# Attention stage of a hybrid trunk: residual input by whole token tiles, output weights two blocks ahead, and a later split of the mixer's tile

## The chip, the cores and the metric

The kernel runs on one core of one Trainium2 chip. The metric is device time in microseconds (us): the median of several executions, lower being better. A profile is one more execution, taken by the hardware profiler. The core's engines are PE (TensorE matmuls, with PEld for its weight loads), DVE (VectorE), ACT (ScalarE), POOL (GpSimd) and SP (SyncE, which here only issues DMAs). Each works through a queue of its own in order and waits at the head of it; POOL issues DMAs too, from between its arithmetic. The clock of PE is granted by a throttle: 1.00 is full speed.

## What is computed

A trunk of two layers over 1024 tokens of width 1024, with 256 context tokens. Layer 0 projects its normalised input, gives eight heads to a two-dimensional neighbourhood attention, which also reads all context keys in the same softmax, and four heads to a bidirectional gated DeltaNet (the "mixer" below). Both halves are gated and go through one output projection:

```python
def even_layer(x, ctx, ...):
    hx, gate_x = adaln_in(x, c_lat, norm_g, mod_w, mod_b)
    px = hx @ w_in
    ...
    na_x = neighbourhood_attention(qx, kx, vx, kc, vc, rpb)
    dn_x, dn_c = bidir_gated_deltanet(px[..., OFF_DN:OFF_AB], ...)
    x_new = x + gate_x * ((jnp.concatenate([na_x, dn_x], axis=-1)
                           * jax.nn.silu(px[..., OFF_Z:])) @ w_out)
```

Per query of the attention:

```python
    s_win = jnp.einsum('bqhd,brqkhd->bhqrk', qr, kw) + bias
    s_ctx = jnp.einsum('bqhd,bkhd->bhqk', qr, kc)
    p = jax.nn.softmax(concatenate([s_win, s_ctx]))
    out = p_win @ v_window + p_ctx @ v_context
```

Layer 1 is a Hyena layer, and a last norm follows. The change lies in the attention of layer 0 and in that half of its output projection, `dn_x @ w_out`, that runs beside it.

## The kernel before

Most products are made of three matmuls of a number's high and low part (hi x hi, hi x lo, lo x hi), so that weights and inputs are split first: `split` casts the high part on ACT and subtracts it from the whole on POOL (or on DVE, where asked) to give the low part.

**The attention stage** is `natten`. It has 64 turns, i = 0 to 63, for 4 pairs of heads, 8 blocks of columns and the 2 heads of a pair; i = 16, 32 and 48 begin pairs 1, 2 and 3. In turn i PE computes the scores of i (`s`, from `nq`, `nkh`, `nkl`), transposes the probabilities of i-2 (`pt`, copied to `pts`), and in odd turns multiplies by the values (`pv`) for i-4 and its predecessor. DVE adds the bias and finds the maximum (line 1050), ACT takes the exponential (line 1051), ACT and DVE finish the result (`nr`, `ny`, lines 1084 to 1086). PE, PEld and DMA issues of a pair are kept in the order of the program; the compiler's scheduler may move other instructions.

**Inputs of a pair.** Per pair two heads' `nq`, `nkh`, `nkl` come in twelve half loads on POOL's DMA queue (line 1012), 0.26 to 0.33 MB each; `nbias` (two of 0.59 MB, line 1007), `bnv` (0.66 MB) and `ny` (0.52 MB) come on SP's. In the program they are issued from the fifth turn of the pair before, two a turn; each goes out once its buffer is free, and `bnv` and `ny` with the first turn of their own pair.

**The filler.** From i = 10 each turn also runs four matmuls of `dn_out`: the mixer's half of the output projection, 8 token tiles x 2 halves of 512 columns x 12 matmuls, all into one PSUM bank `do`. A half tile therefore takes three turns. Tile t's mixer input `dyr` is loaded and split into `dyh` and `dyl` one tile ahead. For a half, `dx` receives x, DVE adds the product (line 1113), and a store writes it back to `xa_d` (line 1114). `dx` is one buffer of 128 x 512, and `dyr` is taken from the ring `wor` of three buffers, which it shares with the raw weights.

**The weights.** `load_wout` brings 16 blocks `ewo_raw` of 128 x 512 (0.26 MB), counted here from 0: a load on SP, a multiply by the gate on POOL (line 1353), and a split. Blocks 0 to 3 come before turn 0, blocks 4 to 7 in turns 0 to 3, and blocks 8 to 15 in odd turns from i = 25 as the program is written; a block's load and its arithmetic are one step. Low parts are made by POOL for blocks 0, 3, 6, ..., by DVE for the others.

The result of the last pair is split into `yeh` and `yel`, which live in the pool `wl` from the stage's start on, empty until then.

Of the kernel before, what the change touches and what calls it, by code (L numbers as in the profile page):

```python
# [10 lines left out]
F32 = mybir.dt.float32  # L11
F32R = mybir.dt.float32r
# [3 lines left out]
ALU = mybir.AluOpType  # L16
# [4 lines left out]
P = 128  # L21
D = 1024
L = 1024
# [5 lines left out]
HEADS = 4  # L29
NTL = 8  # L30
# [31 lines left out]
class Kernel:  # L62
# [192 lines left out]
    def run(self):  # L255
# [45 lines left out]
        with ExitStack() as so, ExitStack() as sh:  # L301
            with ExitStack() as st:
                gate = self.pool(st, "wg").tile([P, D], F32, name="gate0")
                nc.sync.dma_start(gate, self.gate_d[0:1, :].to_broadcast([P, D]))
                wp = self.pool(st, "wo")
                ylp = self.pool(st, "wl")
                yl = [ylp.tile([P, L], F32R, name="ye" + n) for n in ("h", "l")]
                with ExitStack() as s1:
                    w = self.natten(s1, wp, yl, gate)
# [622 lines left out]

    def natten(self, st, wp, yl, gate):
# [21 lines left out]
        half = KT // 2  # L957
        wout = self.load_wout(w, wp, ap["e_w_out"], "ewo", gate,
                              [(k, h) for h in range(2) for k in range(half, KT)] +
                              [(k, h) for h in range(2) for k in range(half)], (None, nc.vector, nc.vector)[:NA_LO])  # L960
        for _ in range(half):
            next(wout)
        self.filler, self.deferred = self.dn_out(w, yp), []
        next(self.filler)
        self.pinned = True
        for i in range(n + 4):
# [18 lines left out]
            if 0 <= i - 4 < n and i % 2:  # L985
                p, j, u = tiles[i - 4]
                self.na_values(p, j, state.pop(i - 5), state.pop(i - 4), *pairs[p])
                if j == 7:
                    _, y = pairs.pop(p)
                    if p < 3:  # L990
                        nc.sync.dma_start(self.y_d[p], y)
                    else:
                        self.split(y, *yl, lo_eng=nc.vector)
        self.drain()
        self.pinned = False
        return w

    def na_unit(self, p, u, nb):

# [85 lines left out]
        nc.vector.tensor_tensor(r3, r3, yj, ALU.mult)  # L1085
        nc.vector.tensor_tensor(yj, po[:, 0, :].rearrange("p (r c) -> p r c", c=8), r3, ALU.mult)

    def dn_out(self, w, yp):

        nc, ap = self.nc, self.ap  # L1090

        def load(i):
            raw = self.wor.tile([P, HEADS, P], F32, name=f"dyr{i}", tag="wor")
            nc.sync.dma_start(raw, self.y_d[HEADS:, :, i * P:(i + 1) * P].rearrange("k p t -> p k t"))
            ys = [yp.tile([P, HEADS, P], F32R, name=f"dy{n}{i}", tag="dy" + n) for n in "hl"]
            self.split(raw, *ys)
            return ys

        nxt = load(0)
        yield  # L1100
        for i in range(NTL):
            ys, nxt = nxt, load(i + 1) if i + 1 < NTL else None
            for n in range(2):
                sl = slice(n * 512, (n + 1) * 512)
                xt = yp.tile([P, 512], F32, name=f"dx{i}_{n}", tag="dx", bufs=1)
                nc.sync.dma_start(xt, ap["x"][i * P:(i + 1) * P, sl])
# [6 lines left out]
                nc.vector.tensor_tensor(xt, xt, ps, ALU.add)  # L1113
                nc.sync.dma_start(self.xa_d[i * P:(i + 1) * P, sl], xt)

# [224 lines left out]
        nc.sync.dma_start(self.g_d[o, cb][:, 16, :], G[:, 0, 8, :])  # L1340


    def load_wout(self, w, pool, ap, name, gate, order, lo_eng=(None,)):

        nc = self.nc
        for n in range(2):
            w.append([pool.tile([P, KT, 512], F32R, name=f"{name}_{p}{n}") for p in ("hi", "lo")])
        for i, (k, n) in enumerate(order):
            sl = slice(n * 512, n * 512 + 512)
            raw = self.wor.tile([P, 512], F32, name=f"{name}_raw{k}_{n}", tag="wor")  # L1350
            nc.sync.dma_start(raw, ap[k * P:(k + 1) * P, sl])
            if gate is not None:
                nc.gpsimd.tensor_tensor(raw, raw, gate[:, sl], ALU.mult)
            self.split(raw, w[n][0][:, k, :], w[n][1][:, k, :], lo_eng=lo_eng[i % len(lo_eng)])
            yield
# [574 lines left out]
```

## Time and profile before

| | us |
|---|---|
| median of 3 runs | 1939.85 |
| lowest and highest of them | 1932.81, 1949.21 |
| the profiled execution | 1935.17 |
| its span in the trace | 1933.1 |
| the attention stage in that span, about | 985 to 1203 |

The mean granted clock of the profiled execution was 0.952. A row of a timeline gives start, length, engine, line, operation, output and inputs, and in square brackets how long the engine stood idle before it and what ended that. `SPq` is SP's queue of DMA issues: such a row is the issue, and the data lands later. Rows of the waits read: who waited, for whom, us in all, times, the longest.

### The profile page before, as it was taken

What the parts mean: (1) busy time and instruction counts of PE and PEld (TensorE: products, weight loads), DVE (VectorE), ACT (ScalarE), POOL (GpSimd) and SP (SyncE); (2) the same over time, 40 slices, a digit from 0 to 9 for tenths busy, and PEclk for the clock granted to TensorE, in tenths of its full rate; (3) what the DMA queues carried; (4) which work ended last, traced back from release to release, by engine and by line L of the source; (5) the groups of instructions that cost most, each with busy time, mean ns of one, the idle gap of its engine ahead of it and who ended that gap; (6) DMA issues with size and microseconds to landing.
All of it is one profiled execution on the core that took longest, in us unless ns stands there. A gap on an engine that the chain in (4) does not pass through costs nothing. (4 is left out here: it accounts for less than half of the span.)

```text
span 1933.1 us, 30413 instructions
## 1 busy us (share of the span) xinstructions
PE 1752.2 (91%) x11156; PEld 1424.3 (74%) x11156; DVE 1373.9 (71%) x2786; ACT 853.3 (44%) x1851; POOL 623.5 (32%) x878
## 2 busy tenths in 40 slices
PE   6798988899988998999987799888999999999998
PEld 2466755688866776788866587767888888888776
DVE  5899998557648643655564466647998998898666
ACT  4566574354535342343353344553344344434421
POOL 0765454422495767701143300330000000000310
PEclk9898988899998999999998899989999999999999
DMA  8545544313433466533499853542433442443434
GB/s 285 172 125 140 164 170 158 120 44 107 141 111 112 152 189 217 179 129 118 170 227 238 190 158 95 170 139 67 121 92 100 100 123 67 119 124 105 123 105 140
DMA packets 133232, 271.05 MB, mean 140 GB/s; under 512 B 44074, under 2 KB 66106, under 8 KB 131035
## 3 DMA queue, kind: packets, MB, share of 16 engines
q1 hardware_dynamic: 123482, 233.45, 37.2%
q0 software_dynamic: 9600, 35.66, 10.0%
q8 instruction: 88, 1.44, 0.3%
q14 instruction: 62, 0.50, 0.1%
HBM read 193.03 MB, written 76.03 MB: 139 GB/s over the span
## 5 line engine op out<-in xcount | busy, mean ns | idle before, releaser
L116 PE MATMUL hx<-h1h,w1x_hi 128*128 128x512 f32 x256 | 101.2, 395 | 0.0
L112 PE MATMUL dn<-hh,wdn_lo 128*128 128x512 f32 (+1 forms) x256 | 95.8, 376 | 5.9 <-POOL wdn_lo L105 5.9
L116 PE MATMUL hx<-h1l,w1x_hi 128*128 128x512 f32 x256 | 100.9, 394 | 0.0
L653 DVE SCALAR_TENSOR_TENSOR dacc<-dpad,convw,dacc 128x1024 f32<-128x1024 f32 (+1 forms) x80 | 83.9, 1079 | 23.9 <-ACT dacc L651 19.5
L116 PE MATMUL hx<-h1h,w1x_lo 128*128 128x512 f32 x256 | 100.7, 393 | 0.0
L756 POOL TENSOR_TENSOR sub<-Lb,Xb 80x31 f32<-80x31 f32 (+15 forms) x124 | 84.2, 679 | 36.5 <-DMA Lb<-lsc_d 18.8
L110 PE MATMUL dn<-hh,wdn_hi 128*128 128x512 f32 (+1 forms) x256 | 95.6, 373 | 0.0
L111 PE MATMUL dn<-hl,wdn_hi 128*128 128x512 f32 (+1 forms) x256 | 95.6, 373 | 0.0
L1051 ACT ACTIVATE pr<-pr,st 128x640 f32<-128x640 f32 (+1 forms) x64 | 51.3, 802 | 73.2 <-DVE st L1050 72.5
L758 POOL TENSOR_TENSOR Xb<-Xb,sub 80x31 f32<-80x31 f32 (+15 forms) x124 | 78.3, 631 | 8.4
L112 PEld LDWEIGHTS dn<-hh,wdn_lo 128*128 128x128 f32 x256 | 49.4, 193 | 14.9 <-POOL wdn_lo L105 6.1
L116 PE MATMUL hu<-h1h,w1u_lo 128*128 128x512 f32 x128 | 51.6, 403 | 4.2 <-DMA w1u_lo<-in_w 4.2
L111 PEld LDWEIGHTS dn<-hl,wdn_hi 128*128 128x128 f32 x256 | 49.3, 193 | 8.0 <-issue 0.5
L110 PEld LDWEIGHTS dn<-hh,wdn_hi 128*128 128x128 f32 x256 | 49.4, 193 | 7.9
L1160 ACT COPY fx<-fx_ps 128x512 f32<-128x512 f32 (+1 forms) x96 | 43.6, 483 | 25.7 <-PE fx_ps L121 22.3
L116 PEld LDWEIGHTS hx<-h1h,w1x_lo 128*128 128x128 f32 x256 | 48.1, 188 | 9.2 <-DMA w1x_lo<-in_w 0.2
L116 PEld LDWEIGHTS hx<-h1l,w1x_hi 128*128 128x128 f32 x256 | 48.2, 188 | 8.9
L116 PEld LDWEIGHTS hx<-h1h,w1x_hi 128*128 128x128 f32 x256 | 48.1, 188 | 8.8
L121 PE MATMUL fx_ps<-ident,ff 128*128 128x128 f32 x288 | 49.5, 298 | 5.6 <-ACT fx L1160 3.6
L1269 PE MATMUL fh<-fhh,w3s 128*128 128x512 f32 x64 | 38.9, 611 | 17.2 <-DVE fh L1271 17.2
L156 POOL DMA_DIRECT2D w1x_lo<-in_w x16 | 13.8, 865 | 124.7 <-ACT w1x_lo L154 124.7
L1293 POOL TENSOR_TENSOR fp<-fh,fh 128x1024 f32<-128x1024 f32 x16 | 39.4, 2464 | 42.3 <-ACT fh L1279 42.3
(571 smaller groups left out, 5980.0 us busy)
## 6 DMA issues: line engine op xcount, KB each, us to landing
hG<-g_d SPq DMA_DIRECT2D x16, 1088.0 KB
g_d<-G SPq DMA_DIRECT2D x16, 1024.0 KB
em_w<-in_em_w SPq DMA_DIRECT2D x24, 512.0 KB
om_w<-in_om_w SPq DMA_DIRECT2D x24, 512.0 KB
wz_raw<-in_w0z SPq DMA_DIRECT2D x16, 512.0 KB
w1x_raw<-in_w SPq DMA_DIRECT2D x16, 512.0 KB
w1x_lo<-in_w POOLq DMA_DIRECT2D x16, 512.0 KB, 7.7
wdn_raw<-in_w0dn SPq DMA_DIRECT2D x12, 512.0 KB
```

The costliest lines, as they stand in the source:

```text
L110: nc.tensor.matmul(ps, wh, xh, start=start, stop=False)
L111: nc.tensor.matmul(ps, wh, xl, start=False, stop=False)
L112: nc.tensor.matmul(ps, wl, xh, start=False, stop=stop)
L116: ins = self.nc.tensor.matmul(*args, **kw)
L121: ins = self.nc.tensor.transpose(out, x, self.ident)
L653: nc.vector.scalar_tensor_tensor(acc[:, t0:t0 + n], pad[:, o + j:o + j + n], cw[:, blk, j:j + 1], acc[:, t0:t0 + n], ALU.mult, ALU.add)
L756: nc.gpsimd.tensor_tensor(tv, Lb[:, j + 1:, j:j + 1].broadcast_to([80, m, c]), Xb[:, j:j + 1, 0:c].broadcast_to([80, m, c]), ALU.mult)
L758: nc.gpsimd.tensor_tensor(Xb[:, j + 1:, 0:c], Xb[:, j + 1:, 0:c], tv, ALU.subtract)
L1051: nc.scalar.activation(pr[:, :n], pr[:, :n], AF.Exp, bias=st[:, 0:1], scale=-1.0, accum_out=st[:, 1:2])
L1160: nc.scalar.copy(out[:, j0:j0 + m, :].rearrange("p a b -> p (a b)"), ps[:, :m * P])
L1269: nc.tensor.matmul(ps, ws[:, od, :], hh[:, sl], start=True, stop=False)
L1293: nc.gpsimd.tensor_tensor(pp[:, :L], hf[:, :L], hb[:, :L], ALU.add)
```

## The change

Four edits, all in the attention stage:

1. `dn_out` loads x by whole token tiles (128 x 1024, 0.52 MB) instead of halves, one tile ahead with the mixer's tile, into two buffers in turn. They are the two of pool `wl`; `yeh` and `yel` take the same two buffers at the end, after the filler has drained. Adds and stores stay by halves.
2. `dyr` has a buffer of its own instead of one of the ring `wor`.
3. The split of the next mixer tile is issued after the first half of the present one, while its load is issued at the tile's start as before.
4. `load_wout` gets `ahead=2`: the load of block k is issued with step k-2. Layer 1's call keeps 0.

```diff
-    def dn_out(self, w, yp):
+    def dn_out(self, w, yp, ylp):
         def load(i):
-            raw = self.wor.tile([P, HEADS, P], F32, name=f"dyr{i}", tag="wor")
+            raw = yp.tile([P, HEADS, P], F32, name=f"dyr{i}", tag="dyr", bufs=1)
             nc.sync.dma_start(raw, self.y_d[HEADS:, ...])
-            ys = [yp.tile([P, HEADS, P], F32R, name=f"dy{n}{i}", tag="dy" + n) for n in "hl"]
+            xt = ylp.tile([P, D], F32, name=f"dx{i}", tag="y" + "eo"[i % 2])
+            nc.sync.dma_start(xt, ap["x"][i * P:(i + 1) * P, :])
+            return raw, xt
+        def split(raw):
+            ys = [yp.tile([P, HEADS, P], F32R, name=f"dy{n}", tag="dy" + n) for n in "hl"]
             self.split(raw, *ys)
             return ys
...
         for i in range(NTL):
-            ys, nxt = nxt, load(i + 1) if i + 1 < NTL else None
+            if i + 1 < NTL:
+                raw, xn = load(i + 1)
             for n in range(2):
-                xt = yp.tile([P, 512], F32, name=f"dx{i}_{n}", tag="dx", bufs=1)
-                nc.sync.dma_start(xt, ap["x"][i * P:(i + 1) * P, sl])
...
-                nc.vector.tensor_tensor(xt, xt, ps, ALU.add)
-                nc.sync.dma_start(self.xa_d[i * P:(i + 1) * P, sl], xt)
+                nc.vector.tensor_tensor(xt[:, sl], xt[:, sl], ps, ALU.add)
+                nc.sync.dma_start(self.xa_d[i * P:(i + 1) * P, sl], xt[:, sl])
+                if n == 0 and i + 1 < NTL:
+                    nxt = split(raw)
+            if i + 1 < NTL:
+                ys, xt = nxt, xn
...
     def load_wout(self, w, pool, ap, name, gate, order, lo_eng=(None,), ahead=0):
+        for kn in order[:ahead]:
+            load(*kn)
         for i, (k, n) in enumerate(order):
+            for kn in order[i + ahead:i + ahead + 1]:
+                load(*kn)
+            raw = raws.pop(0)
...
                     if p < 3:
                         nc.sync.dma_start(self.y_d[p], y)
                     else:
+                        self.drain()
+                        yl = [ylp.tile([P, L], F32R, name="ye" + n, tag="y" + t) for n, t in (("h", "e"), ("l", "o"))]
                         self.split(y, *yl, lo_eng=nc.vector)
```

PE's order is the same before and after. The other queues change in this stage alone. Rows name output and input tiles with a running number, and the shape.

SP, from the middle of pair 0 to the start of pair 1 (`nbias`, `bnv`, `ny` are pair 1's; `dyr_10293` and, after, `dyr_10295` are tile 2's mixer input). Before:

```order
L1007 DMA nbias_9896<-in_na_bias 128x1152
L1007 DMA nbias_9922<-in_na_bias 128x1152
L1094 DMA dyr_10081<-y_d 128x4x128
L1094 DMA dyr_10293<-y_d 128x4x128
L1114 DMA xa_d<-dx_0_10087 128x512
L1106 DMA dx_1_10180<-in_x 128x512
L1020 DMA bnv_10277<-nv_d 128x1280
L1022 DMA ny_10279<-zz_d 128x1024
L1094 DMA dyr_10500<-y_d 128x4x128
```

After:

```order
L1363 DMA ewo_raw_0_9853<-in_e_w_out 128x512
L1363 DMA ewo_raw_0_9875<-in_e_w_out 128x512
L1007 DMA nbias_9900<-in_na_bias 128x1152
L1007 DMA nbias_9926<-in_na_bias 128x1152
L1120 DMA xa_d<-dx_9803 128x512
L1020 DMA bnv_10279<-nv_d 128x1280
L1022 DMA ny_10281<-zz_d 128x1024
L1363 DMA ewo_raw_0_10599<-in_e_w_out 128x512
L1363 DMA ewo_raw_0_10677<-in_e_w_out 128x512
L1120 DMA xa_d<-dx_9803 128x512
L1094 DMA dyr_10500<-y_d 128x4x128
L1097 DMA dx_10297<-in_x 128x1024
```

Weight blocks 8 and 9 (9853, 9875) now stand ahead of pair 1's `nbias`; before, nothing of theirs was there. `bnv` and `ny` follow the first store at once instead of the second half's x load. The load of x tile 2 (10297) stands ahead of block 12 (10753) and behind both stores of tile 0 (`dx_9803`), whose buffer it takes.

POOL, behind the twelve loads of pair 1 (`nq_10422` and the rows like it are pair 2's). Before:

```order
L105 TENSOR_TENSOR ewo_lo_9778<-ewo_raw_1_9849,ewo_hi_9777 128x512
L105 TENSOR_TENSOR dyl_10084<-dyr_10081,dyh_10083 128x512
L105 TENSOR_TENSOR dyl_10296<-dyr_10293,dyh_10295 128x512
L1012 DMA nq_10422<-nq_d 64x1024
L1012 DMA nkh_10423<-nk_d 64x1280
L1012 DMA nkl_10424<-nk_d 64x1280
L1012 DMA nq_10422<-nq_d 64x1024
L1012 DMA nkh_10423<-nk_d 64x1280
L1353 TENSOR_TENSOR ewo_raw_0_10603<-ewo_raw_0_10603,gate_9715 128x512
```

After (the row of three dots leaves out six more of pair 2's loads):

```order
L105 TENSOR_TENSOR ewo_lo_9776<-ewo_raw_1_9823,ewo_hi_9775 128x512
L1375 TENSOR_TENSOR ewo_raw_0_9853<-ewo_raw_0_9853,gate_9715 128x512
L1375 TENSOR_TENSOR ewo_raw_0_9875<-ewo_raw_0_9875,gate_9715 128x512
L105 TENSOR_TENSOR dyl<-dyr_10295,dyh 128x512
L1012 DMA nq_10422<-nq_d 64x1024
L1012 DMA nkh_10423<-nk_d 64x1280
...
L1012 DMA nkl_10454<-nk_d 64x1280
L1012 DMA nq_10452<-nq_d 64x1024
L105 TENSOR_TENSOR ewo_lo_9774<-ewo_raw_0_9875,ewo_hi_9773 128x512
L1375 TENSOR_TENSOR ewo_raw_0_10599<-ewo_raw_0_10599,gate_9715 128x512
L1375 TENSOR_TENSOR ewo_raw_0_10677<-ewo_raw_0_10677,gate_9715 128x512
```

The multiplies of blocks 8 and 9 (9853, 9875) stand right behind pair 1's loads, and block 10's (10599) behind ten of pair 2's, where block 8's stood behind five.

ACT, around the exponentials of i = 14 (`pr_10219` before, `pr_10221` after) and i = 15 (`pr_10243`, `pr_10245`). Before:

```order
L1051 ACTIVATE pr_10219,st_10218<-pr_10219,st_10218 128x512
L1064 COPY pts_10227<-pt_3_10233 128x256
L102 CAST dyh_10295<-dyr_10293 128x512
L1051 ACTIVATE pr_10243,st_10242<-pr_10243,st_10242 128x512
L1064 COPY pts_10251<-pt_3_10257 128x256
```

After:

```order
L1051 ACTIVATE pr_10221,st_10220<-pr_10221,st_10220 128x512
L1064 COPY pts_10229<-pt_3_10235 128x256
L102 CAST ewo_hi_9773<-ewo_raw_0_9853 128x512
L102 CAST dyh<-dyr_10295 128x512
L1051 ACTIVATE pr_10245,st_10244<-pr_10245,st_10244 128x512
L102 CAST ewo_hi_9773<-ewo_raw_0_9875 128x512
```

The cast of block 8's high part stands between the two exponentials, ahead of the mixer's cast, which was alone there.

More of the change, by code (lines that the diff above doesn't have):

```diff
@@ L306, in run @@
                 ylp = self.pool(st, "wl")
-                yl = [ylp.tile([P, L], F32R, name="ye" + n) for n in ("h", "l")]
                 with ExitStack() as s1:
-                    w = self.natten(s1, wp, yl, gate)
+                    w, yl = self.natten(s1, wp, ylp, gate)
                 hp = self.pool(sh, "h1p", side="right")
@@ L930, in dn_finish, with natten @@
         self.defer(FILL_LOAD[min(hd + 1, 3)] - 1, out)
-    def natten(self, st, wp, yl, gate):
+    def natten(self, st, wp, ylp, gate):
         nc, ap = self.nc, self.ap
@@ L959, in natten @@
                               [(k, h) for h in range(2) for k in range(half, KT)] +
-                              [(k, h) for h in range(2) for k in range(half)], (None, nc.vector, nc.vector)[:NA_LO])
+                              [(k, h) for h in range(2) for k in range(half)], (None, nc.vector, nc.vector)[:NA_LO], ahead=2)
         for _ in range(half):
             next(wout)
-        self.filler, self.deferred = self.dn_out(w, yp), []
+        self.filler, self.deferred = self.dn_out(w, yp, ylp), []
         next(self.filler)
@@ L992, in natten @@
                     else:
+                        self.drain()
+                        yl = [ylp.tile([P, L], F32R, name="ye" + n, tag="y" + t) for n, t in (("h", "e"), ("l", "o"))]
                         self.split(y, *yl, lo_eng=nc.vector)
-        self.drain()
         self.pinned = False
-        return w
+        return w, yl
     def na_unit(self, p, u, nb):
@@ L1340, in filter_spectrum, with load_wout @@
         nc.sync.dma_start(self.g_d[o, cb][:, 16, :], G[:, 0, 8, :])
-    def load_wout(self, w, pool, ap, name, gate, order, lo_eng=(None,)):
+    def load_wout(self, w, pool, ap, name, gate, order, lo_eng=(None,), ahead=0):
         nc = self.nc
@@ L1347, in load_wout, with load @@
             w.append([pool.tile([P, KT, 512], F32R, name=f"{name}_{p}{n}") for p in ("hi", "lo")])
+        raws = []
+        def load(k, n):
+            raw = self.wor.tile([P, 512], F32, name=f"{name}_raw{k}_{n}", tag="wor")
+            nc.sync.dma_start(raw, ap[k * P:(k + 1) * P, n * 512:n * 512 + 512])
+            raws.append(raw)
+        for kn in order[:ahead]:
+            load(*kn)
         for i, (k, n) in enumerate(order):
             sl = slice(n * 512, n * 512 + 512)
-            raw = self.wor.tile([P, 512], F32, name=f"{name}_raw{k}_{n}", tag="wor")
-            nc.sync.dma_start(raw, ap[k * P:(k + 1) * P, sl])
+            for kn in order[i + ahead:i + ahead + 1]:
+                load(*kn)
+            raw = raws.pop(0)
             if gate is not None:
```

3 lines of the change are left out of this document (2 added, 1 removed).

## Prediction

> **What bounds the kernel now.** I read the page first, then the windows over the attention stage, the waits in it, and the timelines of PE, SP and POOL.
>
> ```profile
> PE 1752.2 (91%) x11156; PEld 1424.3 (74%) x11156; DVE 1373.9 (71%) x2786; ACT 853.3 (44%) x1851; POOL 623.5 (32%) x878
> ...
> PEclk9898988899998999999998899989999999999999
> DMA  8545544313433466533499853542433442443434
> ```
>
> PE is busy for 91% of the span, so a gain must come from places where PE is not. The DMA row has one nearly full place, slices 21 to 23 (9, 9, 8), about 1015 to 1110 us: the attention stage. In windows (columns: stretch and length, busy time and count of PE, PEld, DVE, ACT, POOL, then granted clock, DMA share, GB/s) it reads:
>
> ```profile
> 985.00:1009.00 24.00, 20.84 (x159) 16.84 (x160) 18.83 (x48) 14.34 (x34) 13.95 (x11) 0.86 0.65 222
> 1009.00:1029.00 20.00, 18.20 (x147) 15.17 (x145) 10.31 (x31) 10.00 (x26) 10.25 (x17) 0.91 1.18 225
> 1029.00:1075.00 46.00, 29.20 (x213) 24.35 (x210) 21.31 (x57) 14.02 (x35) 16.33 (x20) 0.82 0.98 240
> 1075.00:1097.00 22.00, 21.80 (x182) 18.29 (x181) 13.16 (x36) 10.81 (x28) 10.51 (x13) 0.90 0.48 123
> 1097.00:1153.00 56.00, 47.68 (x393) 40.50 (x394) 30.34 (x86) 21.38 (x56) 5.87 (x7) 0.94 0.69 186
> 1153.00:1190.00 37.00, 37.00 (x329) 31.28 (x328) 26.38 (x76) 17.84 (x47) 2.02 (x2) 1.00 0.27 90
> ```
>
> From 1029 to 1075 PE works 29.2 of 46 us while the DMA engines are full at 240 GB/s; by 1153 it is full at clock 1.00. The waits of the stage (us in all, times, longest):
>
> ```profile
> DVE dx L1113 <- DMA dx<-in_x: 28.8, 5, 12.2
> PE do L116 <- DVE dx L1113: 25.3, 5, 10.3
> POOL ewo_raw L1353 <- DMA ewo_raw<-in_e_w_out: 37.9, 10, 15.0
> ACT ewo_hi L102 <- POOL ewo_raw L1353: 10.9, 7, 2.7
> ACT dyh L102 <- PE do L116: 3.7, 5, 0.9
> ```
>
> PE's in-order queue stands 25.3 us behind the residual add, and the add behind a load of x. The five places, after the last matmul ahead of the first:
>
> ```profile
> 1029.61 0.28 PE L116 MATMUL s<-nkl,nq 128*128 128x256 f32 x1
> ...
> 1040.21 0.80 PE L116 MATMUL do<-ewo_hi,dyh 128*128 128x512 f32 x1 [10.32 <-DVE dx L1113]
> ...
> 1073.46 0.80 PE L116 MATMUL do<-ewo_hi,dyh 128*128 128x512 f32 x1 [6.48 <-DVE dx L1113]
> ...
> 1093.75 0.50 PE L116 MATMUL do<-ewo_hi,dyh 128*128 128x512 f32 x1 [0.20 <-DVE dx L1113]
> ...
> 1109.82 0.80 PE L116 MATMUL do<-ewo_hi,dyh 128*128 128x512 f32 x1 [6.74 <-DVE dx L1113]
> ...
> 1137.84 0.51 PE L116 MATMUL do<-ewo_hi,dyh 128*128 128x512 f32 x1 [1.58 <-DVE dx L1113]
> ```
>
> The first is the head of i=16, where pair 1 starts. The cause of it, from SP's and DVE's timelines:
>
> ```profile
> 1020.37 0.33 SPq L1114 DMA_DIRECT2D xa_d<-dx  x1
> ...
> 1031.22 0.35 SPq L1106 DMA_DIRECT2D dx<-in_x  x1
> ...
> 1039.46 0.69 DVE L1113 TENSOR_TENSOR dx<-dx,do 128x512 f32<-128x512 f32 x1 [12.22 <-DMA dx<-in_x]
> ```
>
> There is one `dx` buffer. Its store goes out at 1020.37, the next load only when that has landed, 10.9 us later, and the load takes 8.2 us more; two trips through full DMA engines stand between two half tiles. After each long wait the clock is halved:
>
> ```profile
> 1040.20:1045.10 4.90, 4.89 (x16) 4.12 (x17) 2.95 (x10) 1.09 (x3) 1.17 (x1) 0.50 0.86 300
> 1073.50:1079.20 5.70, 5.70 (x33) 4.64 (x33) 1.80 (x6) 1.29 (x3) 1.27 (x1) 0.50 0.54 155
> 1109.80:1113.40 3.60, 3.58 (x12) 3.11 (x13) 2.38 (x8) 0.92 (x2) 0.00 (x0) 0.50 0.29 111
> ```
>
> **The parts, and their sum.** (a) x by whole tiles, one tile ahead, in two buffers: the load no longer waits for the store just made, but for the one of the tile before. All five waits go: -25.3 us. (b) The 14.2 us at clock 0.50 would be 7.8 at the 0.91 of the window from 1009: -6.4 us. Ends of (a) and (b): 0, if the DMA engines are the true bound, and -31.7.
>
> (c) A new stall at i=17. The first keys of pair 1 come through POOL's queue, the bias and values through SP's:
>
> ```profile
> 1004.03 0.90 SPq L1007 DMA_DIRECT2D nbias<-in_na_bias  x2
> ...
> 1031.62 0.43 SPq L1020 DMA_DIRECT2D bnv<-nv_d  x1
> ...
> 1009.23 0.55 POOL L1012 DMA_DIRECT2D nq<-nq_d  x1
> ...
> 1020.05 0.51 POOL L1012 DMA_DIRECT2D nkl<-nk_d  x1 [1.79 <-DMA nq<-nq_d]
> 1020.58 1.30 POOL L105 TENSOR_TENSOR ewo_lo<-ewo_raw,ewo_hi 128x512 fp32r<-128x512 f32 x1
> ...
> 1028.93 0.54 POOL L1012 DMA_DIRECT2D nq<-nq_d  x1
> ...
> DMA to landing us min/median/max: 11.8/11.8/11.8
> ```
>
> The last row is of the load issued at 1020.05: pair 1's twelve loads end at 1031.85, behind a stall that hid them. In the changed order nbias (1.18 MB) stands on SP behind weight blocks 8 and 9 (0.26 MB each) that were not there, so it moves from 1004 into the time of the twelve loads; bnv and ny come right behind the first store instead of at 1031.6. From 1010.5 the twelve (3.67 MB), nbias, the two blocks, a mixer tile (0.26) and a store (0.26) are 5.9 MB, at 0.24 MB/us 24.6 us: the last key lands at about 1035.5 by this estimate. PE, no longer held at 1029.9, wants it at the head of i=17, about 1031.5. So 4 us, and about 2 for the clock behind it. Ends: 0 (the old 1031.85) and 10 (the whole first stall back, by a path of its own). I take +6, between, since the bytes are counted.
>
> (d) The weights. Blocks 10 to 15 are multiplied by the gate on POOL, cast on ACT in the stretch i=18 to 27, where in the changed order a cast stands ahead of the softmax exponential of the same turn. Their loads share SP's queue with x loads that wait for stores, so SP itself blocks: the load of tile 2 waits for both stores of tile 0, the second landing at about 1042 (1031 + 10.9), and blocks 12 to 15 and pair 2's nbias stand behind it. Before, POOL waited 37.9 us for raw blocks and ACT 10.9 for POOL, all beside other work. Ends: 0 and the 10.9; I take +6, since SP's queue still has these waits and PE is now ahead of them by the 16.8 us of the first two stalls.
>
> (e) At nothing: eight x loads fewer on SP (8 x 0.33 us of issue, SP not on the path); the mixer's split put after the first half, whose ACT cast waited for PE for 3.7 us in five places already, and whose result is needed 12 matmuls later; the two whole x tiles at the start (0.8 MB more before 1009, where the DMA share is 0.65; ends -2 and +2); and the last pair's split, which now waits for the last stores since it takes the x buffers:
>
> ```profile
> 1179.11 0.32 SPq L1114 DMA_DIRECT2D xa_d<-dx  x1
> ...
> 1202.63 1.22 DVE L105 TENSOR_TENSOR yel<-ny,yeh 128x1024 fp32r<-128x1024 f32 x1 [1.11 <-ACT yeh L102]
> ```
>
> Even 10.9 us after it that store has landed at 1190, 12 us ahead of need. The tail keeps its pace, two turns of i in 5.55 us: these rows are four pairs of turns apart, 22.21 us, with PE full, so nothing else can shorten it.
>
> ```profile
> 1152.72 0.29 DVE L1085 TENSOR_TENSOR nr<-nr,ny 128x128 f32<-128x128 f32 x1 [1.36 <-ACT nr L1084]
> ...
> 1174.93 0.29 DVE L1085 TENSOR_TENSOR nr<-nr,ny 128x128 f32<-128x128 f32 x1 [1.19 <-ACT nr L1084]
> ```
>
> Sum: -25.3 - 6.4 + 6 + 6 = -19.7. Against the profiled execution's 1935.17 us (span 1933.1, 2.1 around it) that is 1915.5. That execution is 4.7 under the median of three, 1939.85, inside their spread of 16 us; I add half of it, 2.3: 1918.
>
> A check by bytes: 20 us at 225, 46 at 240 and 22 at 123 GB/s are 18.2 MB from 1009 to 1097. At 240 throughout they take 76 us, so at most 12 of those 88 us can go; the two later stalls with their half clock (6.7 + 1.6 + 1.6) add 10. So -22 is about the floor, which agrees with -19.7 and not with -31.7.
>
> How the two queues share, in 1029:1075 (packets, MB, share of the 16 engines):
>
> ```profile
> q1 hardware_dynamic: 4192, 7.10, 54.5%
> q0 software_dynamic: 1018, 3.87, 43.3%
> ```
>
> POOL's queue q0 gets 43% beside SP's q1. [...]
>
> **Rivals.** *B, the DMA engines bound it.* The stalls of 1029 to 1097 come back as waits for keys, bias or values; only what the later stalls cost goes, about 10. For it: shares of 1.18 and 0.98. Against: 0.48 in 1075:1097, so there is slack just behind. Time: 1935.2 + 2.3 - 10 = 1928.
>
> *C, all is hidden.* The keys land at 1031.85 as before, and the weights' waits stay beside other work: -31.7, 1906. For it: the twelve loads start first in their queue. Against: the bytes.
>
> *D, slower: ACT's order.* ACT's cast of weight block 8 now stands ahead of the exponential of i=15, its multiply on POOL behind all twelve loads of pair 1; block 10's cast stands ahead of that of i=20, its multiply behind ten of pair 2's. POOL has had only eight loads under way at a time, so a slow landing holds the multiply, the cast, the exponential, and then PE. The exponential of i=15 ran here:
>
> ```profile
> 1027.54 0.72 ACT L1051 ACTIVATE pr<-pr,st 128x512 f32<-128x512 f32 x1
> ```
>
> At the pace seen (eleven steps from 1009.23 to 1020.05) the tail of another block (1.3), the multiply (1.3) and the cast (0.6) end at 1023.8, in time. If SP's traffic halves that pace, the twelfth issue comes at 1031 and the cast ends at 1034: 7 us late, and again for pair 2, with 5 of half clock behind both, on top of (c) and (d) and with the first two stalls of (a) not gained (16.8, and 4.8 of clock): -31.7 + 21.6 + 12 + 19 = +21, 1958. It decides when the twelfth issue is later than about 1024. For it: a share over 1. Against: nbias is the only large transfer that moves into that time.
>
> That the change does not do what it says I leave out: the order shows the loads moved.
>
> **Chances.** Mine 0.53, B 0.20, C 0.20, D 0.07. The likeliest one's own range, from (c) and (d) at 9 to 20 in place of 12 and 3 us either way for the runs, is 1909 to 1928. To hold eight in ten it reaches into C and B: 1904 to 1935. A measurement of this kernel tells about 1% from no change: 1920.5 is that bound. Faster: two thirds of mine and 0.9 of C, 0.53; slower: the half of D beyond 1959, 0.04; the rest, with B, 0.43.
>
> **What would show it.** (a): no wait of `do` on the add over 1 us; the add has x long before. (b): no stretch at 0.50 near 1040, 1073 and 1110. (c): a wait of PE's scores at i=17 on the load of nkh or nkl, 3 to 8 us, followed by a low clock. (d): waits of ACT's ewo_hi on POOL of over 2 us each between i=18 and 27, and exponentials late behind them. B shows as scores waiting over 8 us on nkl, nbias or bnv with the DMA share at 1; C as PE full from 1029; D as an exponential at i=15 or 20 behind an ewo_hi cast, with POOL's multiply behind its loads. The forecast is wrong if the windows outside 985 to 1203 move by more than 3 us, which nothing here accounts for.

## The result, and the profile after

The changed kernel took 1914.18 us (median of 4 runs, 1912.35 to 1919.9) against 1940.62 us of the kernel before (4 runs): a ratio of 0.987, 95% interval 0.982 to 0.992. The forecast was 1918. The profiled execution of the changed kernel took 1915.67 us. One execution among the experiments below, of the kernel with two further edits, took 2816.59 us at a mean clock of 0.608 and is left out of its row. The changed kernel's page, from the first two parts:

```profile
PE 1743.7 (91%) x11156; PEld 1422.0 (74%) x11156; DVE 1379.5 (72%) x2786; ACT 853.8 (45%) x1851; POOL 624.6 (33%) x878
...
PEclk9799978899999998999998999999999999999999
DMA  8445544313434367534389854533442443444424
```

PE has the same 11156 matmuls and is busy 8.5 us less (1752.2 before), which fits less time at half clock (the middle's mean clock, below, is 0.95 where it was 0.84). The DMA row is nearly as full there as it was (8, 9, 8 for 9, 9, 8).

The same stretches as before, in windows:

```profile
985.00:1009.00 24.00, 18.09 (x143) 14.08 (x144) 18.13 (x49) 16.36 (x39) 18.40 (x18) 0.93 0.68 227
1009.00:1029.00 20.00, 18.34 (x158) 15.51 (x156) 13.37 (x38) 10.04 (x26) 10.33 (x15) 1.00 1.19 237
1029.00:1075.00 46.00, 36.00 (x284) 29.59 (x285) 25.94 (x64) 17.88 (x44) 18.18 (x19) 0.93 1.00 246
1075.00:1097.00 22.00, 22.00 (x193) 18.89 (x192) 14.68 (x43) 9.57 (x25) 7.49 (x13) 1.00 0.94 217
1097.00:1153.00 56.00, 55.98 (x482) 47.84 (x482) 37.70 (x107) 25.75 (x68) 2.56 (x2) 1.00 0.56 170
```

From 1075 on PE is full at clock 1.00; of the stretches before, 1029 to 1075 has the most time without a matmul, 10 us. Fixed times mix the two kernels' progress, so from here the stage is cut by its own turns: from the exponential of i=0 to that of i=10 (the start), on to that of i=28 (the middle), and on to the last split, `yel` (the tail). Windows with these bounds, first of the kernel before:

```profile
987.63:1013.22 25.59, 22.37 (x162) 17.80 (x162) 19.54 (x52) 16.46 (x40) 18.17 (x19) 0.87 0.68 209
1013.22:1087.48 74.26, 56.24 (x429) 47.44 (x430) 35.52 (x97) 27.52 (x70) 26.21 (x31) 0.84 0.93 213
1087.48:1202.63 115.15, 103.19 (x900) 86.55 (x898) 68.20 (x196) 50.42 (x129) 15.46 (x20) 0.97 0.52 143
```

And of the changed kernel:

```profile
985.21:1009.92 24.71, 19.01 (x148) 14.78 (x149) 18.84 (x49) 16.36 (x39) 19.32 (x20) 0.93 0.70 224
1009.92:1075.41 65.49, 53.83 (x440) 44.73 (x439) 38.80 (x102) 27.92 (x70) 27.59 (x32) 0.95 1.06 244
1075.41:1180.32 104.91, 101.52 (x905) 85.89 (x903) 68.41 (x196) 50.07 (x128) 12.97 (x18) 1.00 0.56 153
```

The stage went from 215.0 to 195.1 us: 0.9 less in the start, 8.8 in the middle, 10.2 in the tail. The span outside it is 1718.1 and 1718.6 us. So the whole difference of these two executions lies in the stage. In the middle the DMA engines run at 244 GB/s with a share of 1.06: 16.0 MB in 65.5 us, where it was 15.8 MB in 74.3.

The waits of the stage now (us in all, times, longest):

```profile
PE s L116 <- DMA nkh<-nk_d: 6.1, 1, 6.1
...
PE do L116 <- DVE dx L1119: 2.6, 2, 1.7
PE s L116 <- DMA nkl<-nk_d: 2.1, 1, 2.1
...
ACT ewo_hi L102 <- POOL ewo_raw L1375: 5.0, 4, 2.0
ACT dyh L102 <- DMA dyr<-y_d: 5.7, 3, 2.8
```

PE's 25.3 us behind the add are 2.6, and the add itself waits for x nowhere: the row of 28.8 us that the kernel before had is gone from the list. A wait of 8.1 us for keys is new. It stands in PE's timeline where the prediction put it, at i=17:

```profile
1033.40 0.55 PE L116 MATMUL s<-nkh,nq 128*128 128x256 f32 x1 [6.06 <-DMA nkh<-nk_d]
1036.03 0.55 PE L116 MATMUL s<-nkl,nq 128*128 128x256 f32 x1 [2.08 <-DMA nkl<-nk_d]
...
1064.48 0.50 PE L116 MATMUL do<-ewo_hi,dyh 128*128 128x512 f32 x1 [1.74 <-DVE dx L1119]
```

The 1.74 us of the last row are no wait for x, although the row names the add. From the timelines of POOL, ACT and DVE:

```profile
1059.61 1.29 POOL L1375 TENSOR_TENSOR ewo_raw<-ewo_raw,gate 128x512 f32<-128x512 f32 x1 [1.56 <-DMA ewo_raw<-in_e_w_out]
...
1060.93 0.62 ACT L102 CAST ewo_hi<-ewo_raw 128x512 fp32r<-128x512 f32 x1 [1.04 <-POOL ewo_raw L1375]
...
1061.58 1.11 DVE L105 TENSOR_TENSOR ewo_lo<-ewo_raw,ewo_hi 128x512 fp32r<-128x512 f32 x1 [1.76 <-ACT ewo_hi L102]
...
1063.76 0.67 DVE L1119 TENSOR_TENSOR dx<-dx,do 128x512 f32<-128x512 f32 x1
```

The load of weight block 13 came late, and the add stood in DVE's queue behind that block's low part; it started without idle time before it. PE's idle time in the middle is 65.5 - 53.8 = 11.7 us: the 8.1 us for keys, these 1.7, 0.9 behind another add that stood in DVE's queue, and 0.9 behind ACT.

Two windows behind the wait for keys show the clock: at half, then partly so, and full from 1040.8 on.

```profile
1033.40:1036.00 2.60, 0.55 (x1) 0.26 (x1) 0.00 (x0) 0.00 (x0) 0.51 (x1) 0.50 1.18 253
1036.00:1040.80 4.80, 4.77 (x36) 3.97 (x36) 1.46 (x4) 0.81 (x2) 1.02 (x2) 0.69 1.26 232
```

The first and last of pair 1's twelve loads in POOL's timeline, and the landing of the last one:

```profile
1006.03 0.55 POOL L1012 DMA_DIRECT2D nq<-nq_d  x1
...
1015.98 0.51 POOL L1012 DMA_DIRECT2D nkl<-nk_d  x1 [1.95 <-DMA nq<-nq_d]
...
DMA to landing us min/median/max: 19.9/19.9/19.9
```

They are issued 3.2 us earlier than before and end at 1035.9, 29.9 us after the first issue instead of 22.6. The two queues between 1009 and 1035, by the view of the DMA queues (packets, MB, share), of the changed kernel:

```profile
q0 software_dynamic: 878, 3.37, 60.2%
q1 hardware_dynamic: 828, 2.78, 58.1%
```

In the kernel before the same stretch read:

```profile
q0 software_dynamic: 1230, 4.71, 98.0%
q1 hardware_dynamic: 1260, 1.01, 19.6%
```

POOL's queue moved 4.71 MB in 26 us before and 3.37 after, because SP's queue, which the old stall had kept nearly empty, now runs beside it; the run with pair 0's bias below tests this. Their shares went from 98.0 and 19.6% to 60.2 and 58.1%.

And SP's timeline has the longest time from a store to the load that needs its buffer:

```profile
1024.55 0.33 SPq L1120 DMA_DIRECT2D xa_d<-dx  x1
1025.10 0.38 SPq L1094 DMA_DIRECT2D dyr<-y_d  x1
1049.26 0.33 SPq L1097 DMA_DIRECT2D dx<-in_x  x1
```

The load of x tile 2, which needs tile 0's last store landed, goes out 24.7 us after that store. What SP's queue moved from 1007.8 to 1049.3:

```profile
q1 hardware_dynamic: 1471, 3.76, 52.8%
```

From 1007.9 to 1025.5 it had been given 3.7 MB (`nbias` 1.18, `bnv` 0.66, `ny` 0.52, two weight blocks, two stores and a mixer tile of 0.26 each). So the store seems to have waited its turn behind these; this is worked out from the two sums, and no run separates it. No add waited for this load, but the last four weight blocks stand behind it in SP's queue.

### The profile page after: what moved, and what is told of

The parts are those of the page before. It is cut to its first block, busy times and chain, and to the rows that moved or that the text cites. A ratio compares the mean times of both kernels' runs of the same rounds, so it can differ in the third digit from the quotient of the medians.

```text
span 1913.7 us, 30399 instructions
## 1 busy us (share of the span) xinstructions
PE 1743.7 (91%) x11156; PEld 1422.0 (74%) x11156; DVE 1379.5 (72%) x2786; ACT 853.8 (45%) x1851; POOL 624.6 (33%) x878
## 5 line engine op out<-in xcount | busy, mean ns | idle before, releaser
L652 DVE SCALAR_TENSOR_TENSOR dacc<-dpad,convw,dacc 128x1024 f32<-128x1024 f32 (+1 forms) x80 | 83.8, 1078 | 23.6 <-ACT dacc L650 19.3
L757 POOL TENSOR_TENSOR Xb<-Xb,sub 80x31 f32<-80x31 f32 (+15 forms) x124 | 86.3, 696 | 8.4
L755 POOL TENSOR_TENSOR sub<-Lb,Xb 80x31 f32<-80x31 f32 (+15 forms) x124 | 76.0, 613 | 35.0 <-DMA Lb<-lsc_d 21.0
L1171 ACT COPY fx<-fx_ps 128x512 f32<-128x512 f32 (+1 forms) x96 | 43.5, 483 | 28.4 <-PE fx_ps L121 24.9
L116 PE MATMUL hu<-h1h,w1u_hi 128*128 128x512 f32 x128 | 51.5, 402 | 0.8 <-ACT hpu L1632 0.8
```

The source lines that it names most:

```text
L116: ins = self.nc.tensor.matmul(*args, **kw)
L652: nc.vector.scalar_tensor_tensor(acc[:, t0:t0 + n], pad[:, o + j:o + j + n], cw[:, blk, j:j + 1], acc[:, t0:t0 + n], ALU.mult, ALU.add)
L755: nc.gpsimd.tensor_tensor(tv, Lb[:, j + 1:, j:j + 1].broadcast_to([80, m, c]), Xb[:, j:j + 1, 0:c].broadcast_to([80, m, c]), ALU.mult)
L757: nc.gpsimd.tensor_tensor(Xb[:, j + 1:, 0:c], Xb[:, j + 1:, 0:c], tv, ALU.subtract)
L1171: nc.scalar.copy(out[:, j0:j0 + m, :].rearrange("p a b -> p (a b)"), ps[:, :m * P])
```

## The experiments

The theory to begin with: two x buffers give the gain; pair 1's keys, slowed by SP's traffic, take part of it back. Rivals: the other edits carry the gain; the DMA engines bound the middle whatever the order. "Ratio" is to the kernel before on the same chip, with its 95% interval (its median on the chips of the experiments was 1936.55, 1936.75 and 1938.17 us); start, middle and tail are those of one profiled execution each, in us, and no kernel was profiled twice.

| kernel | median | ratio (interval) | start + middle + tail |
|---|---|---|---|
| before | 1940.62 | 1 | 25.6 + 74.3 + 115.1 |
| changed | 1914.18 | 0.987 (0.982 to 0.992) | 24.7 + 65.5 + 104.9 |
| x edit alone | 1923.77 | 0.992 (0.989 to 0.995) | 21.9 + 73.8 + 106.3 |
| weights ahead alone | 1941.29 | 1.002 (1.000 to 1.004) | 22.3 + 81.1 + 117.3 |
| changed, weights not ahead | 1910.99 | 0.988 (0.985 to 0.992) | 23.5 + 69.7 + 104.6 |
| changed, split at load | 1918.34 | 0.991 (0.988 to 0.994) | 23.7 + 71.7 + 104.8 |
| changed, x by halves | 1926.3 | 0.994 (0.992 to 0.997) | 27.1 + 71.2 + 106.5 |
| changed, values late | 1922.41 | 0.993 (0.990 to 0.995) | 24.2 + 68.5 + 112.8 |
| changed, inputs from turn 0 | 1916.36 | 0.990 (0.987 to 0.993) | 22.7 + 69.2 + 105.2 |
| changed, cast on POOL | 1917.47 | 0.989 (0.986 to 0.992) | 24.3 + 65.6 + 104.6 |
| changed, both of these | 1920.65 | 0.992 (0.989 to 0.995) | 24.1 + 77.2 + 104.6 |
| changed, pair 0's bias | one run, 1910.16 | | 23.6 + 66.4 + 104.6 |
| changed, pair 0's keys | one run, 1904.77 | | 25.8 + 52.7 + 104.6 |
| changed, six stores left out | one run, 1931.44 | | 25.0 + 72.4 + 104.6 |

The span outside the stage differs between these executions from 1712.4 to 1727.3 us, which is why the stage's parts tell more than single totals. How far the middle differs between executions of one kernel is not known.

**The x edit alone** (`dn_out` as changed, but `dyr` from the ring, split with its load, weights not ahead).

> Only the first edit on the kernel before: x by whole tiles into two buffers; the mixer's tile is in the ring and split with its load, no weights ahead. Theory (this edit carries the whole gain): stage 194 to 201 us (before 215.0, after 195.1), 1911 to 1920. Rival (the other three edits together carry a part): stage 205 or more, 1925 or more.

Stage 202.0, 1923.77 us: between the two theories. The tail has nearly the whole gain (106.3 against 115.1), the middle none. The waits in the middle say why, of ACT for POOL's weight blocks and of POOL for their loads:

```profile
ACT ewo_hi L102 <- POOL ewo_raw L1373: 19.0, 9, 7.1
```

```profile
POOL ewo_raw L1373 <- DMA ewo_raw<-in_e_w_out: 50.2, 10, 15.1
```

ACT waited 5.0 us in the changed kernel. The weights come later here, exponentials stand behind their casts, and PE waited 8.4 us for ACT's copies behind those. Three edits are left out at once; that it is the mixer's tile in the ring of three is likely, but not shown.

**Weights ahead alone** (`load_wout` as changed, on the kernel before).

```diff
-                              ..., (None, nc.vector, nc.vector)[:NA_LO])
+                              ..., (None, nc.vector, nc.vector)[:NA_LO], ahead=2)
```

> The kernel before with only the weight blocks loaded two ahead. Theory (the gain comes from the two x buffers): no gain, waits of do on the add 20 to 30 us as before, stage 212 to 220 us, 1935 to 1945. Rival (the weights' lead carries part): stage under 208, 1930 or less.

No gain, as the theory had it; the stage was 220.8 us, just over its range. PE's waits on x fell from 25.3 to 16.2 us, and this one took their place, as ACT waited for `dyr`:

```profile
PE do L116 <- ACT dyh L102: 12.3, 1, 12.3
```

In the order of this kernel ten weight blocks go out before the mixer's tile 1, where eight did, and that tile's load stands in SP's queue behind the second half's x load, which went out at 1032.97, 18.5 us after the store that it waited for. Whether a buffer of its own for `dyr` would have brought it forward was not tested alone.

**Weights not ahead**, the other three edits kept.

```diff
-                              ..., (None, nc.vector, nc.vector)[:NA_LO], ahead=2)
+                              ..., (None, nc.vector, nc.vector)[:NA_LO])
```

> The changed kernel with the weight blocks not loaded ahead (the other three edits stay). Theory (two x buffers give the gain, about 32 us of waits and half clock; the keys of pair 1 take some of it back): about as the change, 1912 to 1919 us, stage from the first exponential to the last split 195 +- 3 us (before 215.0, after 195.1), wait of the scores at i=17 still 5 to 9 us, perhaps 1 to 2 us shorter because blocks 8 and 9 (0.52 MB) stand behind the bias. Rival (the lead of the weights is part of the gain): POOL waits for raw blocks again as before (37.9 us in the stage) and the exponentials come late for it, stage 200 us or more, 1919 or more.

As the theory had it in the stage (197.8), and in time a little under its range (1910.99). The scheduler brings blocks 8 and 9 forward by itself, to 1003.9 (1003.1 in the changed kernel). The wait for keys was 3.1 + 1.7 us, but a wait of `do` for a weight block, 3.2 us, preceded it. The ratios of this kernel and the changed one overlap: the lead is worth nothing that the times show, though the middle of this one execution is 4.2 us longer.

**The split back at its load.**

```diff
-                raw, xn = load(i + 1)
+                nxt, xn = load(i + 1)
...
-                if n == 0 and i + 1 < NTL:
-                    nxt = split(raw)
```

> The changed kernel with the mixer's split put back to its load. Theory: worth nothing either way, stage 195 +- 2 us, 1912 to 1918; the only trace of it is the ACT cast dyh that waits 2.8 us for its tile ahead of the exponential of i=21, which may come a turn earlier and wait 1 to 3 us longer. Rival (the later split keeps ACT free): casts waiting for dyr in front of exponentials in several places, stage 200 or more.

Stage 200.2 against 195.1, 6.2 us of it in the middle: the rival's size, but not by its mechanism. ACT waited only 0.3 us for `dyr`; it waited for weight blocks, 8.7 us in 4 places, the longest 4.5 (2.0 in the changed kernel). The intervals of this kernel and the changed one overlap, so what the later split is worth is not shown.

**x by halves, in two buffers.**

```diff
+                xt = ylp.tile([P, D], F32, name=f"dx{i}_{n}", tag="y" + "eo"[n])[:, 0:512]
+                nc.sync.dma_start(xt, ap["x"][i * P:(i + 1) * P, sl])
```

> The changed kernel with x loaded by half tiles again, half n into buffer n: two buffers, but a load waits for the store of the half two before, and 2 KB rows. Theory: two buffers are what counts; a store trip and a load were 10.9 + 8.2 = 19.1 us in the full place against six turns of about 16.6, so waits of the add on x come back with 2 to 6 us in all, and since bnv and ny of pair 1 now go out before the weights the wait for keys falls from 8.1 to 3 to 6; stage 193 to 199, 1911 to 1919. Rival (the whole tile one ahead is needed): waits of do on the add over 10 us in all, stage 205 or more.

Stage 204.7, waits of `do` on the add of 9.8 us, of which the add itself waited 7.7 for x: beyond the theory's range and just short of the rival's. The longest:

```profile
1055.36 0.79 PE L116 MATMUL do<-ewo_hi,dyh 128*128 128x512 f32 x1 [5.70 <-DVE dx L1118]
```

In the tail the second buffer is enough (106.5). The middle was 5.7 us longer than with whole tiles; here a wait for x does take part.

**Values late, to free the time of the keys.**

```diff
-                if (j, u) == (0, 0):
+                if (j, u) == ((1, 1) if p else (0, 0)):
```

> The changed kernel with bnv and ny of pairs 1 to 3 (1.18 MB each pair) issued three turns later, so that they don't share the time of the twelve key loads. Theory (SP's traffic slows the keys): the twelve loads of pair 1 end 3 to 5 us sooner after their first issue (29.9 us now), the wait at i=17 falls from 8.1 to 3 to 5 us; what the values then cost at i=21 is open, 0 to 5. Stage 190 to 196. Rival (the DMA engines are the bound, whatever the order): the wait only moves from the scores to the values, stage 195 +- 1. Rival (SP's traffic doesn't slow POOL's loads): the wait at i=17 stays 7 to 9.

The theory failed: the twelve loads still took 28.4 us, the wait at i=17 was 6.4, the stage 205.5. SP's queue still moved 2.30 MB between 1009 and 1035 (2.78 in the changed kernel). Then pair 2's values came late and cost 5.4 us in the tail:

```profile
1108.34 1.97 PE L116 MATMUL pv<-pts,bnv 128*64 128x128 f32 x16 [5.37 <-DMA bnv<-nv_d]
```

**Pair 0's bias for all pairs**, to take 1.18 MB a pair off SP's queue.

```diff
-        bias = nb.tile([P, 1152], F32, name="nbias" + nm, tag="nbias")
+        if p:
+            bias = self.bias0[u]
```

> The changed kernel without the loads of nbias for pairs 1 to 3, which use pair 0's (1.18 MB a pair less on SP's queue; it leaves these loads out and its biases are those of another pair). Theory (SP's traffic in the same time slows the keys): the twelve loads of pair 1 take 24 to 27 us from first issue to last landing instead of 29.9, the wait at i=17 falls from 8.1 to 3 to 6 us. Rival (POOL's queue is as slow by itself, or the keys simply start too late): they still take 28 us or more, wait 7 to 9.

The twelve loads took 25.5 us and the wait at i=17 fell to 4.0 us, both as the theory had it:

```profile
1028.24 0.36 PE L116 MATMUL s<-nkh,nq 128*128 128x256 f32 x1 [2.45 <-DMA nkh<-nk_d]
1030.15 0.47 PE L116 MATMUL s<-nkl,nq 128*128 128x256 f32 x1 [1.56 <-DMA nkl<-nk_d]
...
1053.42 0.44 PE L121 MATMUL pt<-ident,pr 128*128 128x128 f32 x2 [4.29 <-ACT pts L1068]
```

But the middle stayed at 66.4 us. The last row is where it went, and ACT's timeline has the cause, a cast in front of the exponential of i=21:

```profile
1051.15 0.62 ACT L102 CAST dyh<-dyr 128x512 fp32r<-128x512 f32 x1 [5.78 <-DMA dyr<-y_d]
```

**Inputs of the next pair asked for from its first turn**, to have the keys early without leaving any out.

```diff
-NA_NEXT = 2
+NA_NEXT = 0
```

> The changed kernel with the next pair's inputs asked for from the first turn of a pair instead of the fifth. Theory (what is left in the stage is that pair 1's keys come late for a PE that no longer waits for x): pair 1's keys have landed before i=16, the 8.1 us of waits at i=17 and about 2 us of half clock go, stage 183 to 188, 1903 to 1907. Rival (the DMA engines are the bound from 985 to 1075): the same bytes make another wait, at the weights, the values or x, of 6 us or more; stage 192 or more. Rival (POOL's queue in order: weight multiplies behind key loads at the start): the first matmuls of the filler at i=10 wait for their weights, some us.

The first rival's outcome, stage 197.1. The wait for keys fell to 3.1 us, and PE then waited 3.7 and 4.0 us behind ACT's copies. The first of these stood behind a weight block's cast, which waited 4.0 us for POOL's multiply, the second behind the mixer's cast, which waited longer than before:

```profile
1059.02 0.62 ACT L102 CAST dyh<-dyr 128x512 fp32r<-128x512 f32 x1 [7.94 <-DMA dyr<-y_d]
```

**That cast on POOL instead of ACT**, and then both edits together.

```diff
-            self.split(raw, *ys)
+            self.split(raw, *ys, hi_eng=nc.gpsimd)
```

> The changed kernel with the high part of the mixer's tile cast on POOL instead of ACT, so that no exponential stands behind a cast that waits for the tile's load. Theory (when the keys come sooner, ACT's cast of tile 3 waiting for its load is what takes the gain back; in the changed kernel itself it costs about 2.6 us at i=21): the wait of 2.8 us goes, the wait for keys stays 7 to 9 us, stage 190 to 194. Rival (POOL, which issues the key loads in the same queue, is held by the cast instead): the wait for keys grows past 9 us or pair 2's keys come late at i=32, stage 196 or more.

> The last edit together with the next pair's inputs asked for from the first turn. Theory: the two limits named are the only large ones left (8.1 us of keys with 2 of clock, then ACT's cast, 3.7 + 4.0 us of late copies when the keys alone were moved): stage 184 to 190, 1903 to 1909. Rival (the DMA engines are the bound up to 1075): the wait turns up again elsewhere, stage 193 or more.

The cast alone: stage 194.5 of the changed kernel's 195.1, the same, just over the theory's 190 to 194. But the way there is another. The wait for keys, expected at 7 to 9 us, was nearly gone:

```profile
1033.23 0.55 PE L116 MATMUL s<-nkl,nq 128*128 128x256 f32 x1 [0.45 <-DMA nkl<-nk_d]
...
1063.45 0.62 ACT L102 CAST ewo_hi<-ewo_raw 128x512 fp32r<-128x512 f32 x1 [5.07 <-POOL ewo_raw L1375]
```

In this order `nbias` went out at 1015.1 instead of 1007.9, and the twelve loads took 23.9 us instead of 29.9. The exponential of i=21 came 34.8 us after that of i=10 (44.3 in the changed kernel), yet the middle was 65.6 us. ACT's casts waited 17.3 us for weight blocks (5.0 in the changed kernel), the longest, above, in front of the exponential of i=24. PE's idle time in the middle fell from 11.7 to 8.6 us, but its busy time grew from 53.8 to 57.0 as the clock was 0.92 instead of 0.95. The bytes and the rate were the same, 16.0 MB at 244 GB/s.

Together, where 184 to 190 was expected, 205.9, the worst of all with whole x tiles: the wait for the last key was 8.2 us, and PE waited 7.8 us behind the add. That was no wait for x either: DVE stood before the low part of a weight block, whose load POOL had waited for:

```profile
1047.44 1.18 DVE L105 TENSOR_TENSOR ewo_lo<-ewo_raw,ewo_hi 128x512 fp32r<-128x512 f32 x1 [6.46 <-ACT ewo_hi L102]
...
1052.22 0.79 PE L116 MATMUL do<-ewo_hi,dyh 128*128 128x512 f32 x1 [7.84 <-DVE dx L1119]
```

**Pair 0's keys for all pairs**, which prices the keys.

```diff
-        for v in range(2):
+        for v in range(0 if p else 2):
```

> The changed kernel without the loads of nq, nkh and nkl for pairs 1 to 3, which use pair 0's (3.67 MB a pair less; it leaves these loads out and its scores are those of another pair). It prices all that the keys cost. Theory: the wait at i=17 and its half clock go, about 10 us, and the small waits on x and copies between i=19 and 26 with them, 2 to 4 us: stage 181 to 186. Rival (little is due to the keys): stage 190 or more.

The middle, in the windows by turns:

```profile
1013.85:1066.51 52.66, 49.66 (x428) 41.90 (x428) 40.91 (x102) 27.33 (x69) 17.82 (x13) 1.00 0.52 172
```

52.7 us, with PE at 49.7 and clock 1.00: PE's own floor is just below. The stage was 183.0 us, as the theory had it. Here 9.1 MB moved in place of 16.0, and ACT waited 3.2 us for weight blocks (5.0 in the changed kernel). The keys' loads cost the middle 12.8 us, all in all, by these two executions: more than the 10 us of the wait at i=17 with its half clock. The rest is likely what they delay in other queues.

**Without the first six stores**, to see whether the round trip of a store at the head of SP's queue holds the middle.

```diff
-                nc.sync.dma_start(self.xa_d[i * P:(i + 1) * P, sl], xt[:, sl])
+                if i > 2:
+                    nc.sync.dma_start(self.xa_d[i * P:(i + 1) * P, sl], xt[:, sl])
```

> The changed kernel without the six stores of token tiles 0 to 2 (1.57 MB; their rows of xa_d hold x alone, copied at the program's start, so the result leaves out the DeltaNet half for these tokens). The x loads of tiles 2 to 4 then wait for an add and not for a store, and SP's queue is not held behind them; bnv and ny of pair 1 also go out some 20 us earlier, since the order of SP changes. Theory (between i=10 and 28 it is the chain store, landing, next load at the head of SP's queue that takes the gains back, 24.7 us for one store in the changed kernel, which is why 2 MB less of bias gained nothing): i=10 to i=28 takes 54 to 60 us instead of 65.5, with no wait of ACT for a mixer tile. Rival (POOL's keys set it by themselves): the wait at i=17 stays 7 us or more and the stretch 62 us or more.

The theory is not borne out: the middle was 72.4 us, and the wait at i=17 again 8.1. ACT waited for no mixer tile, as forecast, but 11.0 us for weight blocks.

```profile
1045.15 0.55 PE L116 MATMUL s<-nkh,nq 128*128 128x256 f32 x1 [6.92 <-DMA nkh<-nk_d]
1046.90 0.55 PE L116 MATMUL s<-nkl,nq 128*128 128x256 f32 x1 [1.20 <-DMA nkl<-nk_d]
```

POOL issued the twelve loads later in this order: from 1019.68, 0.2 us behind the exponential of i=10, where the changed kernel was 3.9 us ahead of it. They took 27.1 us. So the run doesn't price the stores: an order that brought the keys 4.1 us later came with it.

## Why the prediction was right

The forecast stage was 19.7 us shorter, the measured one 19.9. By its terms:

- **(a) and (b), the waits on x and the half clock.** Right, and shown: no add waits for x any more, where it was 28.8 us. "The two later stalls with their half clock" were put at 9.9 us, the tail lost 10.2, and every kernel with two x buffers and pair 2's values in time has a tail of 104.6 to 106.5. The sign that was named, no wait of `do` on the add over 1 us, failed at 1.74 us, but by a weight block in front of the add and not by x.
- **(c), the new stall.** The mechanism was right, and the bias experiment shows that SP's traffic sets the pace (29.9 to 25.5 us for the loads, 8.1 to 4.0 of waiting); so does the run with the cast on POOL. The landing, 1035.5 forecast and 1035.9 measured, was met by luck: 5.9 MB were counted from 1010.5, without `bnv` and `ny`; the loads began at 1006.0, and 6.9 MB moved before the last one landed. The term was too small: 8.1 us of waiting and about 1.8 for the clock (an estimate: half of 0.55 us and 31% of 4.77 us in the two windows behind the wait), for 4 and 2. PE came to i=17 near 1027.3, not 1031.5, as it had gained 3.9 us by i=15, 2.4 of them before the stage even began.
- **(d), the weights.** A late weight block did reach PE, as forecast, but the term was too large: of the 6 us PE saw 1.7, the wait behind the add. The x load that blocks SP went out even later than forecast, 24.7 us after the store and not 10.9, a row from a time when SP's queue was nearly empty. That this made block 13 late is not shown: its load went out at 1051.97, 2.7 us after that x load, but also only 1.4 us after block 10 had left the buffer of the ring that it takes. ACT's waits for weight blocks fell from 10.9 to 5.0 us; with the x edit alone they are 19.0, so the other three edits keep them small.
- **(e).** The start cost nothing (0.9 gained), the end had `yel` at once, 1.1 us behind its cast as before, and the span outside the stage is the same within 0.5 us. The mixer's split, put at nothing, cost PE 0.9 us: the cast of tile 3 waited 2.8 us for its load in front of the exponential of i=21.
- **The check by bytes** held as a floor, -22. But 240 GB/s is not a limit of the engines: the prediction's own rows have 300 at a share of 0.86, and 1064.4 to 1068 in the changed kernel has 360 at 0.92.
- **The rivals.** C fell at i=17. D's lateness did not occur in the changed kernel; with the inputs from turn 0 it did, 4.0 us for a multiply that stood behind pair 2's loads on POOL. B gave the wrong size, but the wait for keys, 8.1 us at a share over 1, lies just past the line of 8 us that was drawn between (c) and B, and B's mechanism is what the experiments met: with the first limit relieved, the next load took its place (weight blocks, mixer tile, values). Of the kernels that do the whole work none had a shorter middle than 65.5.
- **Slips of reckoning.** 24.6 us from 1010.5 end at 1035.1; the range of the likeliest case begins at 1912, not 1909, by its own terms; slices 21 to 23 are 967 to 1111 us. None changes the forecast.

(c), (d) and (e) cost about 12.5 us in all where 12 were taken. That the sum is this near is luck: one term was too small by 4 us, one too large by about as much. The measured terms give -18.3 (-31.7, 12.5, and 0.9 behind an add in DVE's queue); the other 1.6 us of the 19.9 belong to none of them.

That the other edits share in the gain was not forecast: the x edit alone gives 0.992 and the whole change 0.987, with intervals that overlap a little, and the profiles put the difference, 8.3 us, into the middle. How much each of them carries was not settled. What exactly sets the middle stays open. The wait for keys alone does not: it was 8.1, 4.0 and 0.5 us in three kernels with a middle of 65.5, 66.4 and 65.6. Bytes alone do not: with 2.0 MB less of bias it moved 14.0 MB at 211 GB/s in nearly the same time. In each of these three the longest later wait of a cast on ACT, 2.8, 5.8 and 5.1 us, is for a load that stands in SP's queue behind tile 0's last store, and the exponentials stand behind the casts. That freeing this queue would shorten the middle is not shown.

## What to carry to other kernels

Here a wait for a transfer, removed in a stretch with a DMA share of 0.93 (1.06 after), was in part exchanged for others: in the middle PE's idle time fell from 18.0 to 11.7 us only, in the tail, with a share of 0.52 and 0.56, from 12.0 to 3.4. And a latency read while SP's queue moved little (1.01 MB in 26 us) did not hold when it moved more (2.78 MB): the 10.9 us from the store to the next load of x became 24.7. A row that says that PE waits for an add doesn't say what the add waits for: read the add's own row, and what stands before it in its queue. And look at what the scheduler put ahead of the critical instruction: a cast that waited 5.8 us for a load cost PE 4.3 us behind it, but with that cast off ACT other casts waited instead.

## What was not expected of the hardware

The queue of POOL's loads lost 28% of its bytes in the same 26 us (4.71 to 3.37 MB) while the total rose only from 221 to 237 GB/s.

Sixteen waits of PE of 3.1 to 12.4 us, in ten of these profiles, were each followed by half clock, where a 128x512 matmul of `do` took 0.63 us instead of 0.39. The clock stayed full behind waits of 1.6 us (the kernel before) and 1.7 us (the changed one). In between both were measured: half clock behind 1.9 us (the x edit alone, at 1020.45) and 2.6 us (cast on POOL with inputs from turn 0, at 1004.16), full clock behind 2.4 us (weights ahead alone, at 1023.89). With the cast on POOL, PE ran at 1.00 up to a wait of 2.2 us at 1030.31, and the stretch behind it reads:

```profile
1031.20:1034.00 2.80, 2.35 (x10) 1.88 (x9) 1.66 (x5) 0.81 (x2) 2.80 (x5) 0.50 0.99 377
```

With six stores left out, this one is behind a wait of 3.0 us at 1015.52:

```profile
1015.50:1019.00 3.50, 3.48 (x36) 3.05 (x37) 2.29 (x7) 3.06 (x8) 3.05 (x3) 1.00 0.25 78
```
